# Moving small TensorE steps and one operand split to other points of an attention and feed-forward kernel

## The chip, the cores and the metric

The kernel runs on one core of a Trainium2 chip. The metric is the device time of one execution in microseconds (us). It is taken in several runs, and the median is compared. The kernel before took 1190.72 us as the median of 3 runs, from 1189.71 to 1190.86.

The engines are named as the profile names them: PE is TensorE, with PEld for its weight loads; DVE is VectorE, ACT is ScalarE, POOL is GpSimd, and SP issues most of the transfers.

## The reference, cut to what matters

Two layers are computed on 512 positions of width 1024, in float32. Layer 0 mixes positions by attention with 8 heads in 3 groups, layer 1 by pooling; each is followed by a gated feed-forward network of width 2816.

```python
for i in range(DEPTH):                       # DEPTH = 2
    j = i // N_MIXERS
    if i % N_MIXERS == 0:
        x = x + dilated_attention_mixer(rmsnorm(x, attn_norm[j]), w_qkv[j], w_attn_out[j])
    else:
        x = x + pooling_mixer(rmsnorm(x, pool_norm[j]), ...)
    x = x + swiglu_ffn(rmsnorm(x, ffn_norm[i]), w_ffn_gate_up[i], w_ffn_down[i])
return rmsnorm(x, final_norm)

def dilated_attention_mixer(h, w_qkv, w_out):   # 3 groups (window, dilation): (128,1) (512,4) (2048,16)
    ...                                         # scores * D**-0.5 + ALiBi bias, masked softmax, times v
    wts = jax.nn.softmax(jnp.stack(lses, axis=0), axis=0)
    o = jnp.sum(wts[..., None] * o, axis=0).reshape(B, S, ATTN_WIDTH)
    return o.astype(h.dtype) @ w_out

def swiglu_ffn(h, w_gate_up, w_down):
    gu = h @ w_gate_up
    gate, up = gu[..., :D_FF], gu[..., D_FF:]
    return (jax.nn.silu(gate) * up) @ w_down
```

## The kernel before, in words

**Products.** A float32 operand is carried as two parts, `hi` and `lo`. `split` (L90 to L92) makes them: ACT copies the value into `hi` (L91), DVE subtracts it to get `lo` (L92). A product of 128 by 128 weights is three matmuls, hi by hi, hi by lo and lo by hi (L457 to L459 in `mult`; L628 to L630 where the weights are the moving operand; L325 to L328 in the plain `Product`). Most projections are computed with seven products of half-size blocks in place of eight, in `seven` (attention) and `chained` (feed-forward). One such product is one call of `mult`, 12 matmuls of 128 by 256.

**Hooks.** `seven` and `chained` run their products in a fixed order, and after product number i + 1 they call `behind(i)`: it first pumps the queue of weight loads and splits, then runs the functions given for hook i. The functions are the rest of the work. So the hook number places small PE work between two products.

**Attention.** For each head h the loop runs three `seven` (g = 0, 1, 2: q and k of the three groups), and then, for even h, a fourth `seven` for the values of group 0 of two heads (`VT`), for odd h `values12` for the values of groups 1 and 2 of two heads. The hooks carry the steps of the heads:
- `scores0(h)` and `scores12(h)`: the scores (PE L712; L732 and L736), bias and maximum on DVE (L715, L718; L739, L742, L743), exponentials on ACT (L721, L746).
- `scatter(h)` (DVE L753) writes `far`; `merge(h)` multiplies it with a swap matrix on PE (L765), forms the softmax weights (DVE L767 to L777, ACT L773) and scales the probabilities (DVE L779, ACT L782).
- `turn0(h)`, `turn12(h)` transpose the probabilities on PE (L795, L816) and copy them out (ACT L799, L801, L817; DVE L802, L821). `turn_values(h)` transposes `VT` (PE L685, ACT L686).
- `output(h)`: probabilities times values (PE L834, L833, L840; ACT L836, DVE L843).

`between(h, g)` returns the hooks of the three `seven`; those of the fourth product stand in the loop.

**Feed-forward.** 22 column blocks j of gate and up are made in pairs; `PARTS` groups them as 0-1 (plain), 2-9 and 10-17 (blocks, whose second matmul is again done with seven products) and 18-21 (plain). `strassen_pair` makes one pair with `chained`. Its last steps on ACT and DVE are Silu and the product with up. For blocks of a plain part `keep(j, up)` then splits the gated result into the operand of the second matmul: one ACT and one DVE instruction of 128 by 512. In `chained` three products share one PSUM tile: each is accumulated on the last, after ACT has copied the sum so far (L531 after the first product, L535 after the second, L539 and L547 later).

**Order.** The program is written in this order, and a scheduler then orders each engine's queue and gives out the buffers. On PE the order is the written one; on ACT and DVE steps of neighbouring hooks are interleaved. Each engine works its queue in order.

Of the kernel before, what the change touches and what calls it, by code (L numbers as in the profile page):

```python
# [21 lines left out]
FC = DFF // P  # L22
# [17 lines left out]
NPLAIN = 4  # L40
# [24 lines left out]
def trunk(ctx: ExitStack, tc: tile.TileContext, xT, xN, norms, w_first, w_qk, w_qkp, w_v0, w_v0p, w_v12, w_out, w_pair, w_down, w_dblock, w_pin, w_pgrp,  # L65
# [400 lines left out]
    def seven(T, one, two, scratch, after={}, blocks=False):  # L466


        (unit,), = units.popleft()
        into, left, right = by_block if blocks else in_place, slice(0, 1), slice(1, 2)  # L470

        def again(v):
            return v.unsqueeze(1).to_broadcast([P, 2, H2])

        p1, p26, p45, p73 = ps(), ps(), ps(), ps()

        def behind(i):
            pump()
            for f in after.get(i, ()):
                f()  # L480

        w = part(unit, "b")
        mult(p1[:, :H2], w, 0, T, "11")
        first, sums = scratch("first"), scratch("sums")
        nc.scalar.copy(first[:, :H2], p1[:, :H2])
        behind(0)
        mult(p26[:, :H2], w, 1, T, "21")
        w.done()
        behind(1)
        w = part(unit, "s")  # L490
        mult(p45[:, H2:], w, 0, T, "1")
        behind(2)
        mult(p73[:, :H2], w, 1, T, "3")
        w.done()
        behind(3)
        w = part(unit, "m")
        mult(p26[:, H2:], w, 0, T, "2")
        nc.vector.tensor_add(into(one), p26, again(first[:, :H2]))
        behind(4)
        mult(p73[:, H2:], w, 1, T, "22")  # L500
        w.done()
        if blocks:
            for a in (left, right):
                nc.vector.tensor_add(in_place(sums, a), in_place(p73, a), into(one, right))
        else:
            nc.vector.tensor_add(sums, p73, again(one[:, H2:]))
        behind(5)
        w = part(unit, "l")
        mult(p45[:, :H2], w, 0, T, "4")
        w.done()  # L510
        nc.vector.tensor_sub(into(two), p45, again(sums[:, :H2]))
        nc.vector.tensor_sub(into(one, right), sums[:, H2:], p45[:, H2:])
        behind(6)
# [82 lines left out]
    with tc.tile_pool(name="opool", bufs=1) as opool:  # L596
        early = opool.tile([P, HEADS, S], F32R, tag="o", name="early")
        with tc.tile_pool(name="apool", bufs=1) as apool:
# [78 lines left out]
            VT = []  # L677
# [146 lines left out]
            def output(h):  # L824
# [13 lines left out]
                for r in range(NT):  # L838
# [10 lines left out]
            U = ([(early[:, 2 * k], early[:, 2 * k + 1]) for k in range(K2)]  # L849
                 + [(latev[:, 2 * k], latev[:, 2 * k + 1]) for k in range(2)]  # L850
                 + [(late12[:, 0], late12[:, 1]), tuple(late)])
            H, T, o = {}, {}, []
# [77 lines left out]
            def later(f, *a):  # L930
                return lambda: f(*a)

            def between(h, g):

                if g == 0:
                    if h % 2:
                        return {1: [later(merge, h - 1)]} if h == 1 else {}
                    return {1: [later(output, h - 2)], 2: [later(merge, h - 1)]}
                if g == (2 if h == 1 else 1):
                    turns = [later(turn0, h - 1), later(turn12, h - 1)]  # L940
                    if h % 2 and h > 1:
                        turns.append(later(turn_values, h - 1))
                    return {1: turns, 3: [later(scores0, h)]}
                return {}

            prepare(0)
            for u in range(NF):
# [17 lines left out]
            for h in range(1, HEADS):  # L965
                for g in range(3):
                    if h == 1 and g < NSOLO:
                        for c in range(2):
                            evac(h, 2 * g + c, product(0))
                        for fs in between(h, g).values():  # L970
                            for f in fs:
                                f()
                    else:
                        for c in range(2):
                            QKV[h, g, c] = apool.tile([P, S], F32, name=f"qk{g}{c}")
                        seven(T, QKV[h, g, 0], QKV[h, g, 1], scratch, between(h, g), g == 0)
                if h == 1:
                    whole = opool.tile([P, HEADS, S], F32, tag="o", name="o")
                    o.extend(whole[:, h, :] for h in range(HEADS))
                if h == HEADS - 1:  # L980
                    X[:] = [x_tile(k) for k in range(KC)]
                    for k in range(KC):
                        nc.gpsimd.dma_start(X[k], xN[:, k, :])
                if h % 2 == 0:
                    VT[:] = [apool.tile([P, S], F32, tag=tag, name="vt") for tag in ("row", "o0")]
                    seven(T, *VT, scratch, {0: [later(scores12, h)], 4: [later(scatter, h), later(output, h - 1)],
                                            5: [later(merge, h)]}, True)
                elif h < HEADS - 1:
                    QKV[h // 2, 12, 2] = values12({0: [later(scores12, h)], 4: [later(scatter, h)]})
                else:  # L990
                    QKV[h // 2, 12, 2] = values12({0: [later(scores12, h)], 1: [later(halve, 0), later(halve, 1)],
                                                   2: [later(scatter, h), later(halve, 2), later(halve, 3)],
                                                   3: [later(merge, h)],
                                                   4: [later(give, ("t", k, 0)) for k in range(2)]
                                                   + [later(halve, 4), later(halve, 5)]})
# [32 lines left out]
    with tc.tile_pool(name="fpool", bufs=2) as fpool:  # L1028
# [8 lines left out]
        def keep(j, up):  # L1037
            held["a", j], t = slot("a")
            act[j] = t[:, 0], t[:, 1]
            split(*act[j], up)  # L1040

        def ffn(layer, nxt, lead, row):
# [19 lines left out]
            T = {}  # L1062
# [22 lines left out]
            B, U, late = {}, {}, deque()  # L1085
# [34 lines left out]
            def later(f, *a):  # L1120
                return lambda: f(*a)

            def waiting():
                hooks = {}
                for i in (4, 5, 6):
                    if late:
                        hooks[i] = [late.popleft()]
                return hooks

            def strassen_pair(u, first=None, right=None):  # L1130
                gt = ftile("gt")
                hooks = waiting()

                def act_right():
                    nc.scalar.activation(gt[:, H2:], gt[:, H2:], AF.Silu)
                    nc.vector.tensor_mul(u[:, H2:], u[:, H2:], gt[:, H2:])
                    right()

                if first:
                    hooks.setdefault(2, []).extend([later(give, ("t", k, 1)) for k in range(K2)] + [first])  # L1140
                if right:
                    hooks.setdefault(3, []).append(lambda: nc.scalar.activation(gt[:, :H2], gt[:, :H2], AF.Silu))
                    hooks.setdefault(5, []).append(act_right)
                left = chained(T, gt, u, ftile, K2, inner=True, after=hooks)
                if not right:
                    nc.scalar.activation(gt, gt, AF.Silu)
                    nc.vector.tensor_mul(u[:, H2:], u[:, H2:], gt[:, H2:])
                nc.vector.scalar_tensor_tensor(u[:, :H2], left, -1.0, gt[:, :H2], op0=OP.mult, op1=OP.mult)

            def gate_up(j, ahead):  # L1150
                first, block = next((p[0], p[2]) for p in PARTS if p[0] <= j < p[1])
                u = tmp.tile([P, S], F32, tag="sq", name="u", bufs=3) if block or ahead else ftile("up")
                i, odd = (j - first) // 2, j % 2
                if j < NPLAIN:
                    plain_pair(j, u)
                elif block and odd and j == FC - 1:
                    strassen_pair(u, later(operands, i, U["even"]), later(operands_right, i, u))
                else:
                    strassen_pair(u)
                if j == FC - 1:  # L1160
                    for key in [key for key in held if key[0] == "t"]:
                        give(key)
                if ahead and not block:
                    U["later"] = j, u
                elif not block:
                    keep(j, u)
                elif not odd:
                    U["even"] = u
                elif j == FC - 1:
                    operands_left(i, u)  # L1170
                else:
                    late.extend([later(operands, i, U["even"]), later(operands_right, i, u), later(operands_left, i, u)])
# [303 lines left out]
```

## Time and profile before

| what | value |
|---|---|
| median of 3 runs | 1190.72 us |
| the profiled execution | 1190.77 us |
| its span, first to last instruction | 1187.8 us |
| outside the span (1190.77 - 1187.8) | 3.0 us |
| mean granted TensorE clock | 0.998 |
| attention, heads 1 to 7 | about 55 to 419 us |
| feed-forward of layer 0, pairs 19 to 21 | about 746 to 776 us |
| mean traffic | 173 GB/s |

The page gives busy times of engines over the whole span; a wait of one engine is found in the list of waits, and the place in the timeline. Rows of the timeline have the start and the length in us, the engine, the line, the operation and the tiles. Matmuls are pipelined, so one row lasts longer than the step to the next: the step from start to start is what a matmul costs PE.

### The profile page before, as it was taken

To read this page: it belongs to the slowest core of one execution; us is meant where nothing else is said; L and a number is where in the kernel's file an instruction comes from. 1 tells how busy PE (TensorE), PEld (TensorE's weight loads), DVE (VectorE), ACT (ScalarE), POOL (GpSimd) and SP (SyncE) were. 2 spreads that over 40 slices of the span, in tenths; PEclk is the share of its full clock that TensorE was granted. 3 is DMA by queue.
4 is the path that set the end of the run, shared out by engine and by line. 5 is a ranking of instruction groups with operands and counts; after the bars stand their busy time and mean duration, and the time that the engine had idled before them with its cause. 6 is when DMAs were issued, how large, how long until landed. Compare 5 with 4: busy or idle time off the path is not lost.

```text
span 1187.8 us, 24866 instructions
## 1 busy us (share of the span) xinstructions
PE 1180.1 (99%) x9934; PEld 1119.3 (94%) x9934; DVE 965.5 (81%) x1693; ACT 711.1 (60%) x1243; POOL 168.8 (14%) x170
## 2 busy tenths in 40 slices
PE   9999999999999999999999999999999999999997
PEld 7889999999999988889999999988888999999997
DVE  7978988889797855699988997656879998898875
ACT  6545555455455546647756775675575775676553
POOL 1111211111111002311111111122130111111100
PEclk9999999999999999999999999999999999999999
DMA  8346666665766449857777777798695777777732
GB/s 293 116 104 163 156 155 158 169 162 147 193 158 155 143 142 212 184 118 188 198 193 191 195 184 199 202 265 210 125 198 107 191 193 198 200 193 191 198 93 71
DMA packets 82003, 205.18 MB, mean 173 GB/s; under 512 B 7760, under 2 KB 13024, under 8 KB 81888
## 3 DMA queue, kind: packets, MB, share of 16 engines
q1 hardware_dynamic: 51088, 141.96, 36.5%
q0 software_dynamic: 30512, 61.36, 31.2%
q8 instruction: 77, 1.26, 0.4%
q14 instruction: 38, 0.31, 0.1%
q10 hardware_dynamic: 288, 0.29, 0.1%
HBM read 201.48 MB, written 2.10 MB: 171 GB/s over the span
## 4 chain that ended last, share of the span: by engine, by line
PE 98%; issue 1%; ACT 0%; DVE 0%; POOL 0%; DVEq 0%; POOLq 0%
PE ps L457 20%; PE ps L459 19%; PE ps L458 19%; PE ps L325 9%; PE ps L328 8%; PE ps L326 8%; PE ps L628 2%; PE ps L629 2%; PE ps L630 2%; PE ps L918 2%; PE ps L840 1%; PE ps L712 1%; PE ps L732 1%; PE ps L834 1%; PE ps L833 0%
## 5 line engine op out<-in xcount | busy, mean ns | idle before, releaser
L91 ACT ACTIVATE w<-raw 128x1024 fp32r<-128x1024 f32 x265 | 280.6, 1063 | 175.5 <-PE ps L459 76.3
L92 DVE TENSOR_TENSOR w<-raw,w 128x1024 fp32r<-128x1024 f32 x265 | 322.8, 1221 | 58.6 <-ACT w L91 54.8
L457 PE MATMUL ps<-far,w 128*128 128x256 f32 x896 | 246.6, 275 | 0.3 <-ACT first L531 0.3
L458 PE MATMUL ps<-far,w 128*128 128x256 f32 x896 | 246.5, 275 | 0.0
L459 PE MATMUL ps<-far,w 128*128 128x256 f32 x896 | 246.4, 275 | 0.0
L457 PE MATMUL ps<-near,w 128*128 128x256 f32 x640 | 179.3, 280 | 0.0
L458 PE MATMUL ps<-near,w 128*128 128x256 f32 x640 | 177.1, 277 | 0.0
L459 PE MATMUL ps<-near,w 128*128 128x256 f32 x640 | 177.1, 277 | 0.0
L457 PEld LDWEIGHTS ps<-far,w 128*128 128x128 f32 x896 | 168.2, 188 | 0.5 <-ACT first L531 0.5
L458 PEld LDWEIGHTS ps<-far,w 128*128 128x128 f32 x896 | 168.2, 188 | 0.1
L459 PEld LDWEIGHTS ps<-far,w 128*128 128x128 f32 x896 | 168.2, 188 | 0.0
L325 PE MATMUL ps<-near,w 128*128 128x512 f32 (+1 forms) x332 | 125.6, 379 | 0.0
L328 PE MATMUL ps<-near,w 128*128 128x512 f32 (+1 forms) x332 | 124.9, 376 | 0.0
L326 PE MATMUL ps<-near,w 128*128 128x512 f32 (+1 forms) x332 | 124.9, 376 | 0.0
L457 PEld LDWEIGHTS ps<-near,w 128*128 128x128 f32 x640 | 120.5, 188 | 0.4
L458 PEld LDWEIGHTS ps<-near,w 128*128 128x128 f32 x640 | 120.3, 188 | 0.0
L459 PEld LDWEIGHTS ps<-near,w 128*128 128x128 f32 x640 | 120.3, 188 | 0.0
L172 POOL DMA_DIRECT2D raw<-w_pair x36 | 43.6, 1210 | 293.3 <-DMA raw<-w_pair 112.2
L325 PEld LDWEIGHTS ps<-near,w 128*128 128x128 f32 x332 | 62.3, 188 | 11.6 <-ACT near L91 0.4
L326 PEld LDWEIGHTS ps<-near,w 128*128 128x128 f32 x332 | 62.4, 188 | 11.3 <-DVE near L92 0.2
L328 PEld LDWEIGHTS ps<-near,w 128*128 128x128 f32 x332 | 62.3, 188 | 11.4
L91 ACT ACTIVATE half<-rawhalf 128x512 fp32r<-128x512 f32 x81 | 51.0, 630 | 14.7 <-PE ps L459 12.6
(310 smaller groups left out, 2758.2 us busy)
## 6 DMA issues: line engine op xcount, KB each, us to landing
raw<-w_pair SPq DMA_DIRECT2D x80, 512.0 KB, 5.0
raw<-w_qkp SPq DMA_DIRECT2D x36, 512.0 KB, 4.2
raw<-w_pair POOLq DMA_DIRECT2D x36, 512.0 KB, 7.4
raw<-w_dblock SPq DMA_DIRECT2D x32, 512.0 KB, 4.6
raw<-w_v SPq DMA_DIRECT2D x18, 512.0 KB, 4.6
raw<-w_qkp POOLq DMA_DIRECT2D x18, 512.0 KB, 7.6
rawhalf<-w_pair SPq DMA_DIRECT2D x36, 256.0 KB, 5.2
raw<-w_dblock POOLq DMA_DIRECT2D x16, 512.0 KB, 7.4
```

The costliest lines, as they stand in the source:

```text
L91: nc.scalar.activation(hi, v, AF.Copy)
L92: nc.vector.tensor_tensor(lo, v, hi.bitcast(F32), op=OP.subtract)
L172: nc.gpsimd.dma_start(self.b.rearrange("p (a c) -> p a c", a=2), self.src[:, None, 3 * n:].to_broadcast([P, 2, n]), accum_op=OP.add)
L325: nc.tensor.matmul(self.p[:, cols], w[0][:, s], mh[:, cols], start=self.done == 0, stop=False)
L326: nc.tensor.matmul(self.p[:, cols], w[0][:, s], ml[:, cols], start=False, stop=False)
L328: nc.tensor.matmul(self.p[:, cols], w[1][:, s], mh[:, cols], start=False, stop=self.done == self.n)
L457: nc.tensor.matmul(dst, w.t[0][:, c], th, start=k == 0 and not on, stop=False, skip_group_check=on)
L458: nc.tensor.matmul(dst, w.t[0][:, c], tl, start=False, stop=False, skip_group_check=on)
L459: nc.tensor.matmul(dst, w.t[1][:, c], th, start=False, stop=k == n - 1, skip_group_check=on)
L628: nc.tensor.matmul(o, mh, wh, start=k == 0, stop=False)
L629: nc.tensor.matmul(o, mh, wl, start=False, stop=False)
L630: nc.tensor.matmul(o, ml, wh, start=False, stop=k == K2 - 1)
```

## The change

Four things move; no instruction is added or removed.
- `turn0` and `turn12` of the head before, which shared hook 1 of g = 1, now have a hook each: 0 and 2 for even h, 0 and 3 for odd h. `scores0(h)` goes from hook 3 to hook 4 of g = 1.
- For odd h from 3 on, `turn_values(h - 1)` goes from g = 1 to hook 3 of g = 0, and `merge(h - 1)` comes in at hook 1 of g = 0.
- For even h, `output(h - 1)` goes from the fourth product to hook 2 of g = 2; in the fourth product `scores12` goes from hook 0 to hook 3 and `scatter` from 4 to 6; `merge(h)` leaves it.
- In the feed-forward networks, for j = 18 to 20, `keep` is put off: it is run in hook 1 of the next `strassen_pair` (j = 18 reaches `keep` by another way and stays).

```diff
             def between(h, g):
 
                 if g == 0:
-                    if h % 2:
-                        return {1: [later(merge, h - 1)]} if h == 1 else {}
-                    return {1: [later(output, h - 2)], 2: [later(merge, h - 1)]}
+                    return {1: [later(merge, h - 1)], 3: [later(turn_values, h - 1)] if h > 1 else []} if h % 2 else {
+                        1: [later(output, h - 2)], 2: [later(merge, h - 1)]}
                 if g == (2 if h == 1 else 1):
-                    turns = [later(turn0, h - 1), later(turn12, h - 1)]
-                    if h % 2 and h > 1:
-                        turns.append(later(turn_values, h - 1))
-                    return {1: turns, 3: [later(scores0, h)]}
-                return {}
+                    return {0: [later(turn0, h - 1)], 2 + h % 2: [later(turn12, h - 1)], 4: [later(scores0, h)]}
+                return {} if h % 2 else {2: [later(output, h - 1)]}
...
-                    seven(T, *VT, scratch, {0: [later(scores12, h)], 4: [later(scatter, h), later(output, h - 1)],
-                                            5: [later(merge, h)]}, True)
+                    seven(T, *VT, scratch, {3: [later(scores12, h)], 6: [later(scatter, h)]}, True)
...
             def strassen_pair(u, first=None, right=None):
                 gt = ftile("gt")
                 hooks = waiting()
+                if "keep" in U:
+                    hooks.setdefault(1, []).append(later(keep, *U.pop("keep")))
...
                 elif not block:
-                    keep(j, u)
+                    if NPLAIN <= j < FC - 1:
+                        U["keep"] = j, u
+                    else:
+                        keep(j, u)
```

How the queues change is shown at three places.

PE, the second `seven` of head 2 (names: `s_912` is the probability tile of group 0 of head 1, `near` and `w` are the operands of the products).

```order
 L458 MATMUL ps<-near,w 128x256
 L459 MATMUL ps<-near,w 128x256
+L795 MATMUL ps<-ident,s_912 128x128 x4
 L457 MATMUL ps<-near,w 128x256
 L458 MATMUL ps<-near,w 128x256
```

The four transposes of `turn0` come one product earlier; those of `turn12` (L816), which followed them directly, now stand two products behind them.

DVE, the fourth `seven` of head 2, from the bias of the second scores to the swap of `merge`; before:

```order
L739 SCALAR_TENSOR_TENSOR s_1747<-ps,b_1505 128x4x128
L739 SCALAR_TENSOR_TENSOR s_1747<-ps,b_1505 128x4x32
L92 TENSOR_TENSOR half<-rawhalf,half 128x512
L742 TENSOR_REDUCE st<-s_1747 128x4
L743 TENSOR_SCALAR nm<-st 128x4
L92 TENSOR_TENSOR w<-raw,w 128x1024
L753 TENSOR_TENSOR far<-st,place 128x64
```

and with the change:

```order
L498 TENSOR_TENSOR vt<-ps,first 128x16x16x2
L742 TENSOR_REDUCE st<-s_1820 128x4
L504 TENSOR_TENSOR sums<-ps,vt 128x256
L743 TENSOR_SCALAR nm<-st 128x4
L504 TENSOR_TENSOR sums<-ps,vt 128x256
L188 TENSOR_TENSOR raw<-raw 128x512
L92 TENSOR_TENSOR w<-raw,w 128x1024
L511 TENSOR_TENSOR vt<-ps,sums 128x16x16x2
L512 TENSOR_TENSOR vt<-sums,ps 128x8x16x2
L753 TENSOR_TENSOR far<-st,place 128x64
L189 TENSOR_TENSOR raw<-raw 128x512
L767 TENSOR_TENSOR far<-ps,place 128x64
```

The first two rows of the changed stretch, L739 with one L92 between its two instructions, stand just ahead of those shown. `far` (L753) was written after two other instructions of the `seven`; it now stands behind eight of them (one L92, L498, two L504, L188, another L92, L511, L512), and L767, which needs the swap matmul, almost follows it.

ACT, layer 0's feed-forward, around the first copy (L531) of pair 21; before:

```order
L145 ACTIVATE w<-raw 128x1024
L1146 ACTIVATE gt<-gt 128x512
L146 ACTIVATE w<-w 128x1024
L91 ACTIVATE near<-up 128x512
L531 COPY first<-ps 128x256
L91 ACTIVATE half<-rawhalf 128x512
L535 COPY sums<-ps 128x256
```

and with the change (L1143 is the line that was L1146):

```order
L145 ACTIVATE w<-raw 128x1024
L1143 ACTIVATE gt<-gt 128x512
L146 ACTIVATE w<-w 128x1024
L531 COPY first<-ps 128x256
L91 ACTIVATE near<-up 128x512
L91 ACTIVATE half<-rawhalf 128x512
L535 COPY sums<-ps 128x256
```

The split of `up` and the copy change places. Of both feed-forward networks this is the only pair of instructions whose order differs on ACT, and on DVE none does.

## The prediction

> **What bounds the kernel now.** First the page: the engines' busy time and the chain that ended last.
>
> ```profile
> span 1187.8 us, 24866 instructions
> PE 1180.1 (99%) x9934; PEld 1119.3 (94%) x9934; DVE 965.5 (81%) x1693; ACT 711.1 (60%) x1243; POOL 168.8 (14%) x170
> PE 98%; issue 1%; ACT 0%; DVE 0%; POOL 0%; DVEq 0%; POOLq 0%
> ```
>
> PE is the chain. Nothing moved off another engine counts by itself; only PE waiting, or PE stepping faster or slower, does. Second, of the list of waits of PE's weight loads the two that lie where the change does:
>
> ```profile
> PEld ps L457 <- ACT first L531: 0.5, 1, 0.5
> PEld ps L325 <- ACT near L91: 0.4, 1, 0.4
> ```
>
> PE waits once for the copy L531 and once for the operand that the last `keep` makes; in the attention it waits for no result at all. So what removed waits can gain is capped below 1 us, under 0.1% of the span. Third, PE's steps themselves, in the timeline. First and last row of five undisturbed stretches:
>
> ```profile
> 132.30 0.28 PE L459 MATMUL ps<-near,w 128*128 128x256 f32 x1
> 146.58 0.28 PE L459 MATMUL ps<-near,w 128*128 128x256 f32 x1
> ...
> 178.96 0.28 PE L458 MATMUL ps<-near,w 128*128 128x256 f32 x1
> 192.50 0.28 PE L459 MATMUL ps<-tx,half 128*128 128x256 f32 x1
> ...
> 148.28 0.28 PE L458 MATMUL ps<-near,w 128*128 128x256 f32 x1
> 153.70 0.28 PE L459 MATMUL ps<-tx,w 128*128 128x256 f32 x1
> ...
> 127.50 0.28 PE L458 MATMUL ps<-near,w 128*128 128x256 f32 x1
> 130.09 0.28 PE L459 MATMUL ps<-tx,w 128*128 128x256 f32 x1
> ...
> 260.49 0.28 PE L459 MATMUL ps<-near,w 128*128 128x256 f32 x1
> 261.17 0.28 PE L459 MATMUL ps<-h,w 128*128 128x256 f32 x1
> ```
>
> The same matmul has two speeds. After `scores0` of head 2, 126 steps take 14.28 us, 113.3 ns each. After `scores0` of head 3, 115 steps take 13.54 us, 117.7 ns. After `scores12` of head 2, 46 steps take 5.42 us, 117.8 ns; after the transposes that head 2 makes for head 1, 22 steps take 2.59 us, 117.7 ns; after `output` in the fourth `seven` of head 4, 6 steps take 0.68 us, 113 ns. The slow step begins at an insertion of other PE work and then either ends within some six matmuls or lasts until the next insertion, the same way in all three head pairs. Each slow step costs 4.4 ns.
>
> **The change part by part.** The sum is made against the profiled execution: span 1187.8 plus 3.0 around it, 1190.8 us, which is also the median of the runs (1190.72).
>
> (a) *The split in the feed-forward.* Though four `keep` calls are put off, the queues differ at one place, layer 0 between pairs 20 and 21:
>
> ```profile
> 766.33 0.61 ACT L91 ACTIVATE near<-up 128x512 fp32r<-128x512 f32 x1
> 766.85 0.35 ACT L531 COPY first<-ps 128x256 f32<-128x256 f32 x1
> 767.10 0.63 ACT L91 ACTIVATE half<-rawhalf 128x512 fp32r<-128x512 f32 x1
> 767.64 0.36 ACT L535 COPY sums<-ps 128x256 f32<-128x256 f32 x1
> 766.71 0.28 PE L459 MATMUL ps<-far,w 128*128 128x256 f32 x1
> 767.25 0.39 PE L457 MATMUL ps<-far,w 128*128 128x256 f32 x1 [0.27 <-ACT first L531]
> ```
>
> PE's step from 766.71 to 767.25 is 0.54 us; without the wait it is 0.11, so 0.43 us are lost. The swap starts L531 at 766.33 in place of 766.85, 0.52 us earlier, more than the loss. The split and the half-weight split then end when they do now, and L535 follows at 767.64 as now. Gain 0.43 us; bounds 0 (the later wait for `near` takes it back, since ACT works without a break there) and 0.43.
>
> (b) *The slow step.* Per head pair I count now (the rows' steps and the first few of each stretch): 23 slow steps after the transposes of the even head, 24 and 11 at the start of its first `seven` (estimates: the two products up to `output` and the one up to `merge`), 48 after `scores12`; in the odd head 23 after the transposes and 119 after `scores0`. That is 248, without the short ones. Afterwards every insertion but those at the start of the even head moves. I read the outcomes by the product that follows: where hook 0 or 1 is served ("21" or "1" follows) the slow step stayed; at hook 2, 4 and 5 it ended at once; at hook 3 once each way. By that, the even head keeps 24 and 11, has 24 after `turn0`, none after `turn12`, `scores0` and `output`; the odd head has 24 after `merge` and 36 after `turn0`; `turn_values` (48 matmuls to the next insertion), `turn12` (12) and `scores12` (60), all at hook 3, are even chances. 119 sure and half of 120: 179, which is 69 fewer; three pairs at 4.4 ns: -0.9 us. Bounds: all three end, 129 fewer, -1.7 us; every insertion stays slow until the next (add 24 after `turn12`, 60 and 108 after the two `scores0`, 96 after `output`), 527 in all, 279 more, +3.7 us.
>
> [...]
>
> (c) *More insertions.* The same instructions go in at 13 places per head pair in place of 10.
>
> ```profile
> 126.51 0.60 PE L795 MATMUL ps<-ident,s 128*128 128x128 f32 x4
> 126.94 0.60 PE L816 MATMUL ps<-ident,s 128*128 128x128 f32 x4
> 127.30 0.36 PE L457 MATMUL ps<-near,w 128*128 128x256 f32 x1
> ```
>
> From 126.51 to 127.50 eight transposes and one matmul take 0.99 us. Four L795 take 0.43, so eight and a matmul by themselves take 0.86 + 0.11 = 0.97. An insertion costs 0.02 us; nine more, 0.2 us. Bounds 0 and 0.8: the matmul at 127.30 lasts 0.20 to the next in place of 0.11, 0.09 each if none of that is the transposes' own.
>
> (d) *`merge` of the even head.* Now PE reaches its swap matmul long after `far`:
>
> ```profile
> 249.42 1.05 PE L732 MATMUL ps<-qk,qk 128*128 128x128 f32 x8
> 250.40 0.46 PE L736 MATMUL ps<-qk,qk 128*32 128x32 f32 x32
> 250.79 0.38 PE L457 MATMUL ps<-near,w 128*128 128x256 f32 x1
> 261.29 0.33 PE L765 MATMUL ps<-far,const 128*128 128x64 f32 x2
> 250.93 0.88 DVE L739 SCALAR_TENSOR_TENSOR s<-ps,b 128x512 f32<-128x512 f32 x2
> 252.33 0.81 DVE L742 TENSOR_REDUCE st<-s 128x4 f32<-128x640 f32 x1
> 253.17 0.17 DVE L743 TENSOR_SCALAR nm<-st 128x4 f32<-128x4 f32 x1
> 253.65 1.22 DVE L92 TENSOR_TENSOR w<-raw,w 128x1024 fp32r<-128x1024 f32 x1 [0.30 <-ACT w L91]
> 255.29 0.23 DVE L753 TENSOR_TENSOR far<-st,place 128x64 f32<-128x64 f32 x1 [0.42 <-ACT s L746]
> 257.62 0.69 DVE L498 TENSOR_TENSOR vt<-ps,first 128x512 f32<-128x512 f32 x1
> 258.22 0.68 DVE L188 TENSOR_TENSOR raw<-raw 128x512 f32<-128x512 f32 x1
> 262.16 0.75 DVE L504 TENSOR_TENSOR sums<-ps,vt 128x256 f32<-128x256 f32 x2
> 264.09 0.68 DVE L511 TENSOR_TENSOR vt<-ps,sums 128x512 f32<-128x512 f32 x1
> 264.81 0.41 DVE L512 TENSOR_TENSOR vt<-sums,ps 128x256 f32<-128x256 f32 x1
> ```
>
> L753 ends at 255.52, 5.8 us ahead of L765. Afterwards five products lie between `scores12` and the swap: 1.37 us for the scores, 0.11 for the first matmul after them, 60 steps of 113 to 118 ns: PE arrives 8.3 to 8.6 us after L732 starts. DVE's queue, counted from the same point: the first L739 can start at about 1.2, when L732 is done and its wait served; two L739 at 0.45 and one L92 at 1.15 take it to 3.2; then L498 0.6, L742 0.8, two L504 0.7, L743 0.2, L188 0.6, L92 1.15, L511 0.6, L512 0.4, L753 0.2: 8.45. The two meet. I take a wait of 0.1 us in each of three pairs, 0.3 in all; bounds 0 and 0.75 (a wait of 0.25).
>
> (e) *At no cost.* The second scores of the even head leave the start of the fourth `seven`, where their operands have just been made; but the list of waits has no L732 or L736, so nothing is won. `turn0` needs the scaled probabilities:
>
> ```profile
> 268.89 1.04 DVE L779 TENSOR_SCALAR s<-s,co 128x160 f32<-128x160 f32 x4
> ```
>
> They are done at 269.93, 8.6 us after L765 at 261.29. In the odd head 72 matmuls (8.2 us) and `turn_values` (eight transposes, 0.9 us) will lie between, 9.1 us: covered by PE's own products, with 0.5 us to spare; if that goes, PE waits the difference, in three heads. `output` comes 84 matmuls and `scores0` after `turn0`, over 10 us.
>
> Sum: -0.4 - 0.9 + 0.2 + 0.3 = -0.8; 1190.7 - 0.8 = **1189.9 us**.
>
> **The rivals.**
> *Slow steps everywhere* (b's upper end). The transposes of both heads left the slow step behind them, and `scores0` of the odd head too; that speaks for it, the clean ends after `merge` against it. With the gain of (a) and the costs of (c) and (d): 1190.7 + 3.7 - 0.4 + 0.5 = 1194.5 us.
> *`far` comes late.* The mechanism is DVE's queue: L753 stands behind eight instructions of the `seven`. It decides from the point where L753 ends more than 8.6 us after L732 starts; one L92 that waits for its ACT half pushes it by 1.2 us, and PE stands still for that: three pairs, 3.5 us beyond the sum, 1193.4. For it: (d) leaves no slack. Against it: DVE's own list above has one idle time of 0.3 us for an ACT half, not of 1.2. [...]
> *Nothing moves: the change does not do what it says.* The slow steps come out as many as before and the wait of (a) returns at the end of pair 21, where ACT has no break: 1190.7 + 0.2 = 1190.9.
> *Quick everywhere.* Every moved insertion recovers at once, 35 slow steps remain, 213 fewer: -2.8 - 0.4 + 0.2 = 1187.7.
>
> **How the numbers follow.** Chances: forecast 0.55, nothing moves 0.15, slow everywhere 0.12, `far` late 0.09, quick everywhere 0.09. A measurement of this kernel tells no change from one of about 0.2%, 2.4 us: 1188.3 to 1193.1. Faster 0.09; slower is the two rivals above, less a little for milder forms of them, 0.18; the same 0.73. The forecast's own range is 1189.0 to 1191.3, from (b)'s better end to the median with (d)'s worse end. The range for 8 in 10 takes in half of each outer rival: 1188.0 to 1193.4.
>
> **What would show it right or wrong.** (a): PE's list of waits has no L531. (b): after `scores0` of odd heads PE's steps are 113 ns, so 106 of them in 12 us; after `turn0` 118. (d): a wait of L765 for DVE L753 of at most some 0.2 us. Wrong would be a PE wait over 1 us in the attention, or a step of 118 ns from `scores0` on to `values12`.

## The result, and the profile after

| what | before | changed |
|---|---|---|
| median of 22 runs each, on the same chips | 1190.36 us (1189.71 to 1191.29) | 1188.16 us (1187.50 to 1188.88) |
| ratio, 95% interval | | 0.9983 [0.9977, 0.9989] |
| profiled execution | 1190.77 us, span 1187.8 | 1188.52 us, span 1186.5 |

The change wins 2.2 us, 0.17%. That is inside the 0.2% which the prediction called no change, though the interval excludes a ratio of 1: by it the gain is 1.3 to 2.7 us. Its direction is the forecast one, but the forecast sum was -0.8. The two spans must not be subtracted: the profiled execution of before had 3.0 us outside its span, the 22 runs of the changed kernel 1.7 to 2.6.

The page of the changed kernel: span, busy time, and the shares of the chain that ended last.

```profile
span 1186.5 us, 24872 instructions
...
PE 1179.0 (99%) x9934; PEld 1118.2 (94%) x9934; DVE 965.5 (81%) x1693; ACT 711.5 (60%) x1243; POOL 173.2 (15%) x170
...
PE 99%; issue 1%; DVE 0%; POOL 0%; DVEq 0%; POOLq 0%
```

PE is still the chain, and DVE and ACT do what they did. The list of waits of PE's weight loads (total, times, longest):

```profile
PEld ps L407 <- issue: 1.4, 4, 0.4
PEld ps L898 <- DVE idle L895: 1.2, 1, 1.2
PEld ps L712 <- issue: 0.5, 2, 0.4
PEld ps L918 <- ACT w L912: 0.5, 1, 0.5
PEld ps L325 <- ACT near L91: 0.4, 1, 0.4
```

The row of L531 is gone and no L765 has come. L918 and L898 belong to the start. The queue of ACT at the place of part (a), and the two matmuls on both sides of the product's border there:

```profile
765.50 0.35 ACT L531 COPY first<-ps 128x256 f32<-128x256 f32 x1
765.75 0.63 ACT L91 ACTIVATE near<-up 128x512 fp32r<-128x512 f32 x1
766.28 0.62 ACT L91 ACTIVATE half<-rawhalf 128x512 fp32r<-128x512 f32 x1
766.80 0.36 ACT L535 COPY sums<-ps 128x256 f32<-128x256 f32 x1
```

```profile
765.87 0.28 PE L459 MATMUL ps<-far,w 128*128 128x256 f32 x1
765.99 0.30 PE L457 MATMUL ps<-far,w 128*128 128x256 f32 x1
```

The copy now stands ahead of the split of the gated chunk, and PE's step there is 0.12 us in place of 0.54.

In the attention the difference is in the length of PE's steps. The first and last row of three stretches of the changed kernel: behind `scores0` of head 3 (103 steps), behind `turn12` in head 2 (22 steps), behind `scores12` of head 2 (58 steps).

```profile
181.01 0.28 PE L458 MATMUL ps<-near,w 128*128 128x256 f32 x1
192.68 0.28 PE L459 MATMUL ps<-tx,half 128*128 128x256 f32 x1
...
129.55 0.28 PE L458 MATMUL ps<-near,w 128*128 128x256 f32 x1
132.14 0.28 PE L459 MATMUL ps<-tx,w 128*128 128x256 f32 x1
...
156.42 0.28 PE L458 MATMUL ps<-near,w 128*128 128x256 f32 x1
163.25 0.28 PE L459 MATMUL ps<-h,w 128*128 128x256 f32 x1
```

The first takes 11.67 us, 113.3 ns a step, where before had 117.7 over the same products and one more. The other two take 2.59 and 6.83 us, 117.7 and 117.8 ns. Below, a slow step is one of 115 to 121 ns from start to start between two 128x256 matmuls of the products (those of `values12` among them), counted from 107 to 426 us; a count holds to about a dozen. Before has 818, the changed kernel 461: 357 fewer, at 4.4 ns 1.6 us.

The same sum from one view: the swap matmul of head 1 and that of head 7 stand at the same place of both programs. First before, then the changed kernel, from PE's timeline:

```profile
118.10 0.22 PE L765 MATMUL ps<-far,const 128*128 128x64 f32 x1
...
410.52 0.22 PE L765 MATMUL ps<-far,const 128*128 128x64 f32 x1
```

```profile
118.77 0.22 PE L765 MATMUL ps<-far,const 128*128 128x64 f32 x1
...
409.68 0.22 PE L765 MATMUL ps<-far,const 128*128 128x64 f32 x1
```

292.42 us before and 290.91 after: 1.51 us less. With the 0.42 us of the feed-forward that is 1.9 of the 2.2 us, inside the interval of the gain. This stretch is a finer measure than the time of a run. The swap of head 1 itself stands anywhere from 118.00 to 119.00 us in the profiled executions below, so the start alone moves by 1 us; but kernels with the same order in the attention agree on the stretch to 0.01 us. The table below has it for every run.

### The profile page after: what moved, and what is told of

It is laid out like the page before. It is cut to its first block, busy times and chain, and to the rows that moved or that the text cites. A ratio compares the mean times of both kernels' runs of the same rounds, so it can differ in the third digit from the quotient of the medians.

```text
span 1186.5 us, 24872 instructions
## 1 busy us (share of the span) xinstructions
PE 1179.0 (99%) x9934; PEld 1118.2 (94%) x9934; DVE 965.5 (81%) x1693; ACT 711.5 (60%) x1243; POOL 173.2 (15%) x170
## 4 chain that ended last, share of the span: by engine, by line
PE 99%; issue 1%; DVE 0%; POOL 0%; DVEq 0%; POOLq 0%
PE ps L457 20%; PE ps L459 20%; PE ps L458 20%; PE ps L325 9%; PE ps L328 8%; PE ps L326 8%; PE ps L628 2%; PE ps L630 2%; PE ps L629 2%; PE ps L918 2%; PE ps L840 1%; PE ps L712 1%; PE ps L732 1%; PE ps L834 1%; PE ps L833 0%
## 5 line engine op out<-in xcount | busy, mean ns | idle before, releaser
L92 DVE TENSOR_TENSOR w<-raw,w 128x1024 fp32r<-128x1024 f32 x265 | 323.0, 1222 | 47.2 <-ACT w L91 43.2
L457 PE MATMUL ps<-far,w 128*128 128x256 f32 x896 | 246.5, 275 | 0.0
L457 PE MATMUL ps<-near,w 128*128 128x256 f32 x640 | 180.2, 282 | 0.0
L457 PEld LDWEIGHTS ps<-far,w 128*128 128x128 f32 x896 | 168.2, 188 | 0.1
L457 PEld LDWEIGHTS ps<-near,w 128*128 128x128 f32 x640 | 120.3, 188 | 0.4
```

The source lines that it names most:

```text
L92: nc.vector.tensor_tensor(lo, v, hi.bitcast(F32), op=OP.subtract)
L457: nc.tensor.matmul(dst, w.t[0][:, c], th, start=k == 0 and not on, stop=False, skip_group_check=on)
```

## Experiments

Each ratio is against runs of before on the same chip; "slow" counts slow steps as defined above, and "swap to swap" is the stretch between the swap matmuls of heads 1 and 7 (292.42 us before, 290.91 with the whole change), both in one profiled execution.

| run | median, us | before there | ratio, 95% interval | slow | swap to swap, us |
|---|---|---|---|---|---|
| keep alone | 1189.94 | 1190.31 | 0.9997 [0.9989, 1.0006] | 816 | 292.42 |
| attention alone | 1188.77 | 1190.31 | 0.9985 [0.9977, 0.9994] | 461 | 290.91 |
| scores of odd heads moved | 1190.38 | 1190.31 | 1.0001 [0.9993, 1.0010] | 817 | 292.42 |
| turn12 of even heads at hook 3 | 1188.35 | 1190.31 | 0.9982 [0.9973, 0.9991] | 430 | 290.74 |
| weights 0 columns off | 1197.58 | 1190.04 | 1.0063 [1.0050, 1.0076] | 1715 | 299.97 |
| weights 28 columns off | 1197.91 | 1190.04 | 1.0065 [1.0053, 1.0078] | steps of 114 to 126 | 300.39 |
| weights 36 columns off | 1196.72 | 1190.04 | 1.0055 [1.0041, 1.0068] | steps of 115 to 121 | 299.29 |
| odd heads' split alone | 1188.02 | 1190.04 | 0.9986 [0.9977, 0.9995] | 370 | 290.40 |
| merge one product earlier | 1191.66 | 1190.01 | 1.0011 [1.0002, 1.0020] | 487 | 294.49 |
| odd heads' split and keep | 1187.88 | 1190.01 | 0.9981 [0.9973, 0.9990] | 373 | 290.40 |
| the same, output earlier | 1187.27 | 1190.01 | 0.9975 [0.9966, 0.9985] | 265 | 289.92 |
| without the odd heads' part | 1188.65 | 1190.01 | 0.9988 [0.9979, 0.9997] | 680 | 291.81 |

### The two parts apart

Keep alone: before, with only the lines of the change in `strassen_pair` and `gate_up`.

> The kernel before with only the feed-forward part of the change (the splits of the gated chunks put off by one product); the attention is that of before. Theory: the 0.43 us that PE loses in front of the product behind copy L531 in layer 0 are won and nothing else moves, so the time falls by 0.45 us to about 1189.9 (before: 1190.36), and the attention keeps its 818 steps of 115 to 120 ns between 107 and 426 us. Rival 1: the whole 2.2 us of the change come from the feed-forward, in waits that the list does not show: 1188.2. Rival 2: ACT works without a break there and the wait comes back elsewhere: 1190.4.

Attention alone: the changed kernel with `keep(j, u)` called at once again.

> The changed kernel with its splits put back as before, so that only the attention differs from before. Theory: three head pairs with fewer steps of 118 ns win 1.6 us (818 such steps before, 461 after, 357 fewer at 4.4 ns), and 0.1 us goes to the added insertions: about 1188.7. Rival 1: the attention's order is worth nothing and the two kernels differ elsewhere (about 1 us of the difference lies outside the span in the two profiled executions): 1190.4. Rival 2: the two parts help each other (a sum that is not additive): 1188.2 or 1189.5.

Keep alone wins 0.37 us by the medians. Its interval holds zero; its list of waits has lost the row of L531, like the changed kernel's, and its 816 slow steps are those of before. Attention alone wins 1.54 us with the 461 slow steps of the whole change. The two sum to 1.91, so neither part needs the other, and the rivals that put everything into one part fall.

### Does the place decide the step?

The prediction read the outcome of an insertion from the hook and the product that follows. Two runs move one insertion each. The first, on before:

```diff
-                    return {1: turns, 3: [later(scores0, h)]}
+                    return {1: turns, 3 + h % 2: [later(scores0, h)]}
```

> The kernel before with one edit: the first scores of odd heads are inserted behind the fifth product of their seven, not behind the fourth. Theory (the place decides whether PE falls back to the quick step): the stretches of 115 to 119 slow steps behind the scores of heads 3, 5 and 7 vanish, 345 steps at 4.4 ns, 1.5 us: about 1188.9, with some 470 slow steps left. Rival 1: it is not the place that makes it quick but what was inserted before (split transposes in the changed kernel): the 118 ns steps stay, 12 fewer in each stretch, 1190.2. Rival 2: the slow step costs nothing in the end, because PE catches up at a later wait: slow steps gone but 1190.4.

PE's timeline of this run behind `scores0` of head 3, the same products as in the first stretch above:

```profile
181.04 0.28 PE L458 MATMUL ps<-near,w 128*128 128x256 f32 x1
...
193.17 0.28 PE L459 MATMUL ps<-tx,half 128*128 128x256 f32 x1
```

103 steps take 12.13 us, 117.8 ns. The same insertion at the same hook leaves 113 ns in the changed kernel and 118 ns here. The place does not decide; my theory fell, and rival 1 (what was inserted before) stands. The second run, on the changed kernel:

```diff
-                    return {0: [later(turn0, h - 1)], 2 + h % 2: [later(turn12, h - 1)], 4: [later(scores0, h)]}
+                    return {0: [later(turn0, h - 1)], 3: [later(turn12, h - 1)], 4: [later(scores0, h)]}
```

> The changed kernel with one edit: the second transposes of an even head's predecessor are inserted behind the fourth product, as in odd heads, not behind the third. Theory (the place decides): the 22 slow steps behind them vanish in three heads, 66 steps, 0.3 us: about 1187.9. Rival (the kind of insertion in the even head decides, the transposes stay slow wherever they stand): 10 of 22 slow steps remain up to the scores, 0.15 us, 1188.0; told apart by the steps in the trace, 113 or 118 ns, since the times are too near each other.

Behind `turn12` of even heads 10 slow steps stand in each of three heads, all there is up to the scores, while at the same hook in the odd heads 3 are slow and 7 quick. Again the rival is right: 430 slow steps in place of 461, and a time that cannot be told from the changed kernel's.

### What in the change makes the odd heads quick?

On before, the odd heads' transposes in two points, everything else as it was:

```diff
                     if h % 2 and h > 1:
-                        turns.append(later(turn_values, h - 1))
+                        return {0: [turns[0], later(turn_values, h - 1)], 3: turns[1:], 4: [later(scores0, h)]}
                     return {1: turns, 3: [later(scores0, h)]}
```

> The kernel before with the odd heads' transposes alone in two points (first transposes and values behind the first product, second transposes behind the fourth, scores behind the fifth), all else as before. Theory (the step in which PE arrives at the scores is carried through them; the split lets PE arrive quick): the stretches of 34 and 114 slow steps of the run with the scores alone moved vanish in heads 3, 5 and 7, some 400 of 818 slow steps left, 1.8 us, 1188.5. Rival (the other moved insertions ahead of it, merge and the scores of the even head, are needed too): over 700 slow steps, 1190.3.

1188.02 us and 370 slow steps: by the medians this piece alone brings what the whole attention part brings. From swap to swap it brings more, 2.02 us against 1.51. The opposite, the changed kernel with `turn0`, `turn12`, `turn_values` and `scores0` of odd heads put back to hooks 1 and 3:

> The changed kernel with the transposes, values and scores of the odd heads put back as before; the changed even heads, merge and the put-off splits stay. Theory (the whole gain in the attention is the odd heads' split; the even heads' part loses 91 slow steps, 0.4 us, about what the put-off splits win): 1190.3, with 800 to 950 slow steps. Rival (the even heads' part makes PE arrive quick in the odd heads too, so that the split there is not needed): 1188.5 or less, with under 500.

680 slow steps and 1188.65 us lie between theory and rival. Where the steps are is in PE's timeline, behind `scores0` of head 3 and of head 5, which the program treats alike:

```profile
179.28 0.28 PE L457 MATMUL ps<-near,w 128*128 128x256 f32 x1
192.42 0.28 PE L459 MATMUL ps<-tx,half 128*128 128x256 f32 x1
...
281.55 0.28 PE L458 MATMUL ps<-near,w 128*128 128x256 f32 x1
295.10 0.28 PE L459 MATMUL ps<-tx,half 128*128 128x256 f32 x1
```

116 steps in 13.14 us are 113.3 ns; 115 steps in 13.55 us are 117.8 ns. Head 3 came to its scores with 113.3 ns steps, heads 5 and 7 with 117.8. So I took the mean of the four steps ahead of `scores0` and of sixteen behind it in all three odd heads of the eleven kernels that leave the weights' place alone. In 11 cases PE arrives slow, and leaves slow in all 11; in 22 it arrives quick, and leaves quick in all 22. `scores0` of an odd head passes on the step it finds. In all but one of the 33 the quick arrivals have the transposes split and the slow ones have not; only head 3 of this last run parts the two, quick with the transposes together. In even heads `scores0` leaves quick whatever it finds (25 arrive slow, 8 quick); why the two differ is open. So is why head 3 arrives quick here and heads 5 and 7 slow. Their weights lie in other buffers of the ring (`BUFS`, five for `w`), and no run holds the buffers fixed; in the other ten kernels the three odd heads go alike all the same.

### Is it the chip's instruction queue, or the memory?

The feed-forward, whose weights stand at another column, has hardly any slow steps: 5 of some 1,500 between 500 and 700 us. Three runs of the changed kernel move only the weights of the attention's sevens against a line of 64 columns (`LINE` in the kernel), from 16 columns to 0, 28 and 36. The edit for 0 is shown; the others put `APART` and `LINE - APART` in its place:

```diff
-    def pairs(*srcs, shift=LINE // 4, back=False):
+    def pairs(*srcs, shift=0, back=False):
```

> The changed kernel with the split weights of the attention's seven-product units placed 0 columns from a 64-column line of SBUF in place of 16, where the feed-forward's weights stand. Theory A (the slow step is a phase between the weight load and the moving operand's read, which the two addresses decide): the number of 118 ns steps between 107 and 426 us changes by more than half from 461, to below 200 (0.01 us per two steps: 1187.0 or less) or above 1000 (1190.6 or more). Theory B (the slow step is the sequencer's, whatever the addresses): 430 to 490 slow steps, 1188.2.

> As the run before, but 28 columns from the line, where the weights of the odd heads' second values stand. Theory A (addresses decide): the count of 118 ns steps changes by more than half from 461; if all vanish the kernel is 2.1 us faster, 1186.1. Theory B (sequencer): 430 to 490 of them, 1188.2.

> As the run before, but 36 columns from the line: the distance between weights and moving operands then is that of the feed-forward, where no 118 ns step is seen. Theory A (addresses decide): the 461 slow steps vanish, 2.1 us, 1186.1. Theory B (sequencer): 430 to 490 of them, 1188.2.

All three are 8.6 to 9.8 us slower than the changed kernel, and from swap to swap 8.4 to 9.5 us. The written order is the same and the lists of waits show no new wait, so the place of the weights in SBUF changes the length of the step, as Theory A has it. But no offset tried was better than 16, and 36, which has the feed-forward's distance, did not bring the feed-forward's step of 113.4 ns. And these runs do not show what chooses between the two steps at offset 16, where both stand in one program at one offset. With 0 nearly every step is 120 ns, where 16 has 113.3 or 117.7; with 28 the steps go round about 114, 121, 120, 125, 120. The groups of weight loads show a trace of the difference. First the changed kernel from 157 to 163 us (slow steps), then from 182 to 192 us (quick), then offset 0 from 184 to 194 us, and last offset 28 in the same window; the last number ahead of the idle time is the mean of one, in ns.

```profile
L457 PEld LDWEIGHTS ps<-near,w 128*128 128x128 f32 x10 | 1.9, 192 | 0.0
L458 PEld LDWEIGHTS ps<-near,w 128*128 128x128 f32 x10 | 1.9, 188 | 0.0
L459 PEld LDWEIGHTS ps<-near,w 128*128 128x128 f32 x10 | 1.9, 188 | 0.0
```

```profile
L457 PEld LDWEIGHTS ps<-near,w 128*128 128x128 f32 x16 | 3.0, 188 | 0.0
L459 PEld LDWEIGHTS ps<-near,w 128*128 128x128 f32 x16 | 3.0, 188 | 0.0
L458 PEld LDWEIGHTS ps<-near,w 128*128 128x128 f32 x16 | 3.0, 188 | 0.0
```

```profile
L457 PEld LDWEIGHTS ps<-near,w 128*128 128x128 f32 x16 | 3.1, 192 | 0.0
L458 PEld LDWEIGHTS ps<-near,w 128*128 128x128 f32 x16 | 3.1, 192 | 0.0
L459 PEld LDWEIGHTS ps<-near,w 128*128 128x128 f32 x16 | 3.1, 192 | 0.0
```

```profile
L458 PEld LDWEIGHTS ps<-near,w 128*128 128x128 f32 x16 | 3.0, 189 | 0.0
L457 PEld LDWEIGHTS ps<-near,w 128*128 128x128 f32 x16 | 3.0, 189 | 0.0
L459 PEld LDWEIGHTS ps<-near,w 128*128 128x128 f32 x16 | 3.0, 189 | 0.0
```

In a quick stretch every load takes 188 ns; in a slow one the load that begins a new block of weights (L457) takes 192; with offset 0 all do. So the loads tell the two steps at offset 16 apart. They do not account for the time: one load in three is 4 ns longer where every step is, and with offset 28 the loads take 189 ns while the steps are 120 ns in the mean. Whether the phase between load and read that Theory A supposes is behind the effect of the place, no run shows.

### How near is `far`?

The changed kernel with `merge` of even heads at hook 0 of the next seven:

```diff
-                    return {1: [later(merge, h - 1)], 3: [later(turn_values, h - 1)] if h > 1 else []} if h % 2 else {
+                    return {0: [later(merge, h - 1)], 3: [later(turn_values, h - 1)] if h > 1 else []} if h % 2 else {
```

> The changed kernel with the even head's merge behind the first product of the next seven in place of the second: PE reaches the swap matmul L765 twelve steps (1.4 us) earlier, while DVE's queue up to L753 stays as it is. In the changed kernel L753 ends 0.4 us before L765. Theory (DVE's queue sets when far is there, so the changed kernel's merge stands within half a microsecond of a stall): L765 waits 1.0 us for L753 in each of three pairs, 2.9 us in all, 1191.1. Rival (PE has room there that the trace does not show): no wait, 1188.2.

Its list of waits begins with

```profile
PEld ps L765 <- DVE far L753: 3.3, 3, 1.1
```

and the time is 3.5 us above the changed kernel's. DVE's queue sets when `far` is there, as the prediction had it. In the changed kernel itself, DVE and then PE of head 4:

```profile
264.63 0.41 DVE L512 TENSOR_TENSOR vt<-sums,ps 128x256 f32<-128x256 f32 x1
264.96 0.22 DVE L753 TENSOR_TENSOR far<-st,place 128x64 f32<-128x64 f32 x1
```

```profile
265.59 0.33 PE L765 MATMUL ps<-far,const 128*128 128x64 f32 x2
```

L753 ends at 265.18, 0.41 us ahead of L765. The twelve instructions of the changed DVE list start there in the order of the list, from L498 at 260.15 to L767 at 265.96 us.

### A faster mix

The odd heads' split together with the put-off splits, on before's even heads:

> The kernel before with the odd heads' transposes in two points and the scores behind the fifth product (as in the run with these alone, 370 slow steps, 1188.02), and with the put-off splits of the feed-forward. Theory: the two gains add, 0.45 us more: 1187.6, below the changed kernel's 1188.2, since the changed even heads cost 91 slow steps, 0.4 us. Rival (the even heads' part of the change is worth something that the slow steps don't show): 1188.0 or more, no better than the changed kernel.

And the same with `output` of the odd head at hook 1 of the fourth seven:

```diff
-                    seven(T, *VT, scratch, {0: [later(scores12, h)], 4: [later(scatter, h), later(output, h - 1)],
+                    seven(T, *VT, scratch, {0: [later(scores12, h)], 1: [later(output, h - 1)], 4: [later(scatter, h)],
```

> The kernel of the run before with the output of the odd head behind the second product of the fourth seven in place of the fifth. Theory (any insertion draws the step anew, and output in the middle of an even head left it quick in both orders): the 47 slow steps after the second scores end after some 11, three times 36 at 4.4 ns, 0.5 us: 1187.1. Rival (output keeps what it finds, as the odd heads' scores did): 47 slow steps and more stay, 1187.6 or up to 0.4 more.

The first, 1187.88, is no better than the changed kernel as far as the intervals tell. The stretch from swap to swap decides: 290.40 us against 290.91, so what else the change moves in the attention costs 0.51 us. In the second, PE behind `scores12` of head 2 and then behind `output`:

```profile
148.29 0.28 PE L458 MATMUL ps<-near,w 128*128 128x256 f32 x1
149.47 0.28 PE L459 MATMUL ps<-h,w 128*128 128x256 f32 x1
...
153.53 0.28 PE L459 MATMUL ps<-near,w 128*128 128x256 f32 x1
155.91 0.28 PE L459 MATMUL ps<-near,w 128*128 128x256 f32 x1
```

Ten steps of 118 ns, then 21 of 113: `output` ends the slow stretch after 11 steps in place of 47, in all three heads. At 1187.27 us it has the lowest median measured, 0.6 below the run beside it and 0.9 below the changed kernel, though its ratio's interval overlaps the changed kernel's; from swap to swap it is 0.48 and 0.99 us shorter than these two.

## Why the prediction came out as it did

- **(a), forecast -0.43:** -0.42 in the trace (a step of 0.54 us became 0.12), -0.37 in the run by itself. Its better end held: ACT still works there without a break, in the four rows above, but no later wait took the gain back.
- **(b), forecast -0.9:** -1.6. This term is the step that failed. The mechanism was right, two step lengths (113.3 and 117.7 ns) of which the longer lasts; it was incomplete in that the slow step also begins without any insertion, where `values12` hands over to the next `seven` (113 ns on L628 to L630, 118 from L457 on, in both kernels). What failed is the rule that the outcome can be read "by the product that follows". The largest single outcome came true, the 119 slow steps behind `scores0` of odd heads went; that was luck as far as the rule goes, since the same insertion at the same hook stays slow when only the scores move. The sign that PE would step at 118 ns after `turn0` did not come. Per head pair:

| insertion in the changed kernel | slow steps forecast | measured, three pairs |
|---|---|---|
| odd: `merge`, hook 1 | 24 | 2 to 3 |
| odd: `turn_values`, hook 3 | 24 (half of 48) | 3 |
| odd: `turn0`, hook 0 | 36 | 1 to 2 |
| odd: `turn12`, hook 3 | 6 (half of 12) | 3 |
| even: `turn0`, hook 0 | 24 | 1 |
| even: `turn12`, hook 2 | 0 | 22 |
| even: `scores12`, hook 3 | 30 (half of 60) | 58 |

  The misses partly cancel in the even heads, to 27 more than forecast, and add in the odd ones, to some 80 fewer: 92 in place of 144, so 119 fewer than before where 69 were forecast. The runs with one insertion moved show why no such rule could work: the same insertion at the same hook comes out either way, and behind `scores0` of odd heads it follows what PE arrived with, in 33 cases of 33. Even one order came out differently in the heads of one execution.
- **(c), forecast +0.2:** about +0.1. Added up step by step between the two swap matmuls, what the product steps take above 113.36 ns each (the mean step of the feed-forward from 500 to 700 us) fell from 3.54 to 1.92 us, 1.62 less; 1.51 are won, so all else, nine more insertions among it, takes 0.11 us more.
- **(d), forecast +0.3:** 0, its lower bound; L753 comes 0.41 us before L765, in all three pairs. The count of DVE's queue was 0.3 us too long (8.45 us after L732 starts; it ends 8.1 after). The rival of the late `far` named the right queue, but its point was not reached. Its price, a `L92` that waits 1.2 us for its ACT half, was not tested: the 1.1 us a pair of the run with `merge` earlier come from PE arriving 1.4 us sooner with 0.4 us to spare.
- **(e), at no cost:** no wait of PE for `turn0` or `output` has appeared.

By its sum the prediction was 1.7 us too high. Of that, 0.7 is (b), 0.3 is (d), 0.1 is (c), and 0.36 is that before itself measured 1190.36 beside the changed kernel and 1190.72 ahead of it; the rest is not accounted for. 1188.16 lies only 0.16 us above the lower edge of the wide range and below the forecast's own 1189.0: the rival *quick everywhere*, given 0.09, came nearest, and it was not everywhere.

## What to carry to other kernels

Where PE never waits, measure start to start by stretches: a matmul can have two step lengths in one program, here 113.3 and 117.7 ns, 4% apart, and the mean hides it. To compare orders that differ by less than the runs do, measure between two instructions that stand at the same place of both programs. Treat the place of weights in SBUF as a tuning size of its own, here worth 8.6 to 9.8 us, over three times more than any order tried. Do not forecast the step behind an insertion from its place; try the order, and read the stretch behind it.

## What the runs showed of the hardware

- A 128x256 matmul with a weight load of its own had these steps in the attention's sevens: 113.3 and 117.7 ns with the weights 16 columns off a line; 120 ns on the line; a round of about 114, 121, 120, 125 and 120 ns 28 columns off it; 115 to 121 ns 36 columns off it. The feed-forward, whose weights stand on the line too, steps at 113.4 ns, so the offset of the weights alone does not set the step.
- The two steps at 16 columns are both stable, over 100 matmuls and more, through borders of products (103 steps of 113.3 ns in the changed kernel, 115 of 117.8 ns in the run without the odd heads' part). The longer one goes with a weight load of 192 ns in place of 188 in every third load, too little to account for 4.4 ns in each.
- Which of the two holds depends on what came before: one program gave 113.3 ns in head 3 and 117.8 ns in heads 5 and 7 for the same order of instructions, and moving only what stands ahead of an insertion changed the step behind it (817 slow steps with the scores of odd heads alone moved, 370 with the transposes ahead of them split too). What chooses is not known.
